# A closing stretch kept in written order: the last blocks of an encoder layer's output stage on four engines

## The chip, the cores and the metric

The kernel runs on one core of a Trainium2 chip. Its engines work side by side, each through its own list of instructions in order: TensorE (PE; its weight loads are PEld), VectorE (DVE), ScalarE (ACT), GpSimd (POOL) and SyncE (SP), which here only issues DMA transfers. Engines wait for one another by semaphores. The metric is the device time of one execution in microseconds (us), the median of several. All times of the trace are in us from the start of the span.

## The reference

One layer of a bidirectional encoder is applied to two sequences of 2048 tokens, 1024 features each, in float32, with shared weights:

```
u = rmsnorm(h, g_norm);  q, k, v, ga, f, gf = split(u @ w_in)
a  = gqa(rope(rmsnorm(q)), rope(rmsnorm(k)), v) * silu(ga)     # 8 q heads, 2 kv heads, 64 wide
fo = (real(fft2(f)) per channel group @ w_fmix) * silu(gf)
h  = h + concat(a, fo) @ w_out
gate = sigmoid(rmsnorm(h, g_ple) @ w_ple_gate)
y  = rmsnorm(h + (p @ w_ple) * gate, g_final)
```

The last three lines are the output stage, and the change is in it.

## The kernel before, in words

Each float32 operand is kept as a high and a low float16 part, and a product is three matmuls per 128 rows of depth: high by high, high by low, low by high (`SPLIT3`). A product of 1024 rows of depth is so a group of 24 matmuls into one bank of PSUM, 128 x 512.

The program first makes the projections, then the attention (`attention`), unit by unit, and between its pieces `interleave` takes pieces of a second stream, `fill`: the rest of the Fourier branch, and then the output stage (`outp`), whose work on the early blocks needs only attention that is already done. A stream is a Python generator; what it yields is the estimated length of the piece it has just written, or `None` for "nothing to be written now". While `interleave` runs, `self.dq` is a list of deferred small steps, written out later by `flush`; when the attention has ended, all of them are written, `self.dq` becomes `None`, and the rest of `fill` is written at once by `drain`.

The output stage works by blocks of 128 tokens, t = 0 to 31 (16 per sequence). For block t there are, by names used from here on:

- the load: `ag` (L1531 and L1532 from the attention's store `agd`, L1533 from the Fourier branch's store `fod`), the gating product on GpSimd (L1535), then the mix as float16, high part `mh` on ScalarE (L1549), low part on VectorE (L1554), and transposes of the Fourier half by DMA, `mT` (L1550). The old features `h` come by L1541.
- out(t,0) and out(t,1): a group of 24 each, `mh` and `mT` against `w_wo`; VectorE adds each to `h` (L1570).
- the norm: `middle(t)` takes the squares of block t and of block t−2 on ScalarE (L1670), one short chain on VectorE gives both roots (L1676 to L1679), then the high part `h_hl` (L1699, ScalarE) and the low part (L1703, VectorE) are transposed by DMA into `hT` (L1700, L1705). Block t−2 gets its last product (L1689) and is stored.
- gate(t,0) and gate(t,1): a group of 24 each, `hT` against `w_pg`; ScalarE's tanh (L1583) reads it.
- emb(t,0) and emb(t,1): the embedding's products, six matmuls, `pT` against `wp`, and two VectorE steps with the tanh (L1592, L1594). They are kept in a list `todo` when the tanh is written, and `embed` writes them at a place inside a later group.

In the interleaved part two groups run at once on half the array each (L1649, tiles of 64 rows): `slot` gives a group its second half beside the next group's first (`halves`). For t >= `WHOLE` = 30, `slot` is called with `whole` true and the group runs alone on the full array (`mm`, L504). A whole group that stands beside a half one is followed by `seen` (L1610), a copy of one column of the half group's bank on VectorE, on which the second half group then waits.

PSUM has eight banks: `ps_f` one, `ps_g` two, and five for the attention, which become `ps_x` when the pool `psD` opens after the attention. `group_bank` takes `ps_x` where that pool is open and `ps_g` otherwise.

The order of instructions on each engine is that of the program text where `tc.manual_schedule` names the engine; elsewhere a scheduler of the language sets it. Before the change, `interleave` runs under a manual schedule for PE, ACT, DVE and SP, and `drain` under the scheduler. GpSimd is under the scheduler in both.

Of the kernel before, what the change touches and what calls it, by code (L numbers as in the profile page):

```python
# [45 lines left out]
_E = mybir.EngineType  # L46
# [119 lines left out]
class Build:  # L166
# [1349 lines left out]
    def outp(self, pool0, ow, open_pool):  # L1516
# [87 lines left out]
        def slot(up, whole):  # L1604


            low = held.pop() if held else None
            def seen():
                j = st.tile([128, 1], F32, name="seen")
                nc.vector.tensor_copy(j[:], low[0][:, 0:1])  # L1610

            if low is not None and low[4] and not whole:
                seen()
            if up is not None and not whole:
                up = (self.group_bank(), *up, not started)
                started.append(True)
                held.append(up)
                yield from halves(up, low)
                return
            if up is not None:  # L1620
                ps = self.group_bank()
                for i, us in enumerate(self.mm(ps[:], up[0], up[1])):
                    yield us
                    yield from embed(i >= 6)
                if low is not None:
                    seen()
                yield from self.after(ticket)
                yield from end(up[2](ps))
            if low is not None:
                yield from halves(None, low)  # L1630

        def embed(now=False):

            if todo and (now or self.dq is None or self.step % 8 in (1, 2, 7)):
                todo.pop()()
                yield 1.48

        def end(more):
            if more is not None:
                todo.append(more)  # L1640
                yield from embed()

        def halves(up, low):
            i = n = 0
            for k in range(8):
                for ia, ib in SPLIT3:
                    for g, sl, a, z in ((up, slice(0, 64), i == 0, False), (low, slice(64, 128), False, i == 23)):
                        if g is not None:
                            nc.tensor.matmul(g[0][:], g[1](ia, k)[sl], g[2](ib, k)[sl], start=a, stop=z,  # L1649
                                             skip_group_check=True)  # L1650
                    i += 1
                    if i in STOPS:
                        yield 0.216 * (i - n)
                        n = i
                        yield from embed(i >= 18)
            yield from self.after(ticket)
            n = self.nflush
            more = low[3](low[0]) if low is not None else None
            yield 0.216 * (24 - STOPS[-1])
            yield from end(more)  # L1660
            if self.dq is not None and self.nflush == n:
                yield None
# [133 lines left out]
        for t in range(N2 + 2):  # L1796
            pr = prep(t + 1) if ok(t + 1) else iter(())
            if ok(t):
                yield from along(slot(out1(t, 0), t >= WHOLE), pr)
                if t == 1:  # L1800
                    yield from middle(0)
                yield from along(slot(out1(t, 1), t >= WHOLE), pr)
                if t == N2 - 2:
                    free.append(True)
                load_p(t)
                M.pop(t)
            if ok(t - 1):
                yield from wait(tk, t - 1)
                yield from along(slot(out3(t - 1, 0), t >= WHOLE), pr)
            if t:  # L1810
                yield from middle(t)
            if ok(t - 1):
                yield from along(slot(out3(t - 1, 1), t >= WHOLE), pr)
            if ok(t + 1):
                if ok(t - 3):
                    yield from wait(t4, t - 3)
                load_x(t + 1)
                yield from pr
                yield from self.after(tm.pop())
# [30 lines left out]
    def run(self):  # L1850
        nc, tc, a = self.nc, self.tc, self.a
# [91 lines left out]
        def fill():  # L1943
            self.nw2k = NW
            self.small = C0 = fill_stack.enter_context(pool("C0", side="right"))
            with pool("B", side="right") as B:
                self.bd = B.tile([128, 2, 512], F32, name="bd")
                ow = {}

                def wload(n, k, pool):  # L1950
                    if k == 0:
                        w = pool.tile([128, 2, 8, 512], F16, name="w_" + n, tag="w16")
                        ow[n] = [w[:, b] for b in range(2)]
                    for b in range(2):
                        nc.sync.dma_start(ow[n][b][:, 2 * k:2 * k + 2, :], self.wd[n][:, b, 2 * k:2 * k + 2, :])

                wl = [lambda n=n, k=k, p=p: wload(n, k, p)
                      for n, p in (("wo0", WP), ("wo1", WP), ("pg0", WP1), ("pg1", WP)) for k in range(4)]
                self.WF.clear()

                calls = []

                def hook(n=1):
                    calls.append(n)
                    for _ in range(n if n > 1 else len(calls) % 2 if len(calls) > 4 else 0):
                        if wl:
                            wl.pop(0)()

                out, go = iter(()), None
                for us in self.fourier2(B, hook):  # L1970
                    if us == "half":
                        out = self.outp(C0, ow, lambda: fill_stack.enter_context(pool("C", side="right")))
                        continue
                    go = go or next(out, None)
                    yield us
                hook(16)
            while not go:
                yield None
                go = next(out)
            yield from out  # L1980

        with tc.manual_schedule(engines={_E.PE, _E.Activation, _E.DVE, _E.SP}):
            f = fill()
# [1 line left out]
        self.step = 10 ** 9  # L1985
        att_stack.close()
        with pool("psD", 5, space=PSUM) as self.psX:
            self.drain(f)
        fill_stack.close()
        w_stack.close()  # L1990

# [52 lines left out]
```

## Time and profile before

| | |
|---|---|
| median of 3 runs | 2601.84 us (2595.85, 2601.84, 2603.52) |
| profiled execution | 2597.87 us, of which the span is 2595.8 us |
| TensorE busy | 2511.0 us, 97% of the span |
| VectorE, ScalarE, GpSimd busy | 1668.4, 1183.6, 1896.6 us |
| granted TensorE clock, mean | 0.991 of full speed |
| part that is no longer interleaved | from about 2507 us to the end |

A row of a timeline has start, duration, engine, line, operation, the tile written and those read, sizes, a count, and in brackets the engine's idle time just before it and what ended it. Equal instructions that follow each other are one row. Matmuls are pipelined: one lasts longer than the distance to the next. L12 is line 12 of the kernel before; in the changed kernel lines from 1608 on stand three or four further down.

### The profile page before, as it was taken

To read this page: it belongs to the slowest core of one execution; us is meant where nothing else is said; L and a number is where in the kernel's file an instruction comes from. 1 tells how busy PE (TensorE), PEld (TensorE's weight loads), DVE (VectorE), ACT (ScalarE), POOL (GpSimd) and SP (SyncE) were. 2 spreads that over 40 slices of the span, in tenths; PEclk is the share of its full clock that TensorE was granted. 3 is DMA by queue.
4 is the path that set the end of the run, shared out by engine and by line. 5 is a ranking of instruction groups with operands and counts; after the bars stand their busy time and mean duration, and the time that the engine had idled before them with its cause. 6 is when DMAs were issued, how large, how long until landed. Compare 5 with 4: busy or idle time off the path is not lost. (4 is left out here: it accounts for less than half of the span.)

```text
span 2595.8 us, 49879 instructions
## 1 busy us (share of the span) xinstructions
PE 2511.0 (97%) x19896; PEld 1384.0 (53%) x19896; DVE 1668.4 (64%) x2382; ACT 1183.6 (46%) x1983; POOL 1896.6 (73%) x1646
## 2 busy tenths in 40 slices
PE   6999989999999999999999999999999999999988
PEld 3566656666656545545545555445544554545533
DVE  7766576777566856566666666666666665766534
ACT  4433353434235545554544545444544444445522
POOL 0465545475659978888888888878887988888840
PEclk9999999999999999999999999999999999999999
DMA  8467588787377742223222233422223322233232
GB/s 259 101 175 198 162 223 230 185 195 180 103 197 248 212 118 62 58 76 78 59 69 75 71 81 88 90 69 63 73 73 82 72 75 63 66 82 76 78 76 53
DMA packets 450265, 297.92 MB, mean 115 GB/s; under 512 B 294000, under 2 KB 394480, under 8 KB 450032
## 3 DMA queue, kind: packets, MB, share of 16 engines
q1 hardware_dynamic: 437952, 256.28, 38.9%
q0 software_dynamic: 12080, 38.46, 4.2%
q8 instruction: 155, 2.54, 0.4%
q14 instruction: 78, 0.64, 0.1%
HBM read 146.12 MB, written 82.45 MB: 88 GB/s over the span
## 5 line engine op out<-in xcount | busy, mean ns | idle before, releaser
L1325 POOL TENSOR_TENSOR acc<-acc,p 128x1024 f32<-128x1024 f32 x384 | 927.6, 2416 | 109.5 <-ACT p L1320 84.6
L1320 ACT ACTIVATE p<-ps_s,s_scale 128x512 f32<-128x512 f32 x1024 | 648.1, 684 | 636.4 <-PE ps_s L1317 613.9
L1355 DVE TENSOR_REDUCE a_mx<-ps_m 128x1 f32<-128x1024 f32 x498 | 608.9, 1223 | 512.0 <-PE ps_m L1347 501.0
L1649 PE MATMUL ps_g<-w_pg,hT 64*128 64x512 f16 x2784 | 494.1, 376 | 3.8 <-DVE seen L1610 2.4
L1383 PE MATMUL ps_o<-p,v 128*64 128x256 f32 x4096 | 468.2, 381 | 0.0
L1317 PE MATMUL ps_s<-q,k 64*128 64x512 f16 x3072 | 433.1, 378 | 1.4 <-ACT p L1320 1.0
L1383 PEld LDWEIGHTS ps_o<-p,v 128*64 128x64 f32 x4096 | 283.7, 137 | 160.4 <-issue 28.5
L504 PEld LDWEIGHTS <-uc 128*128 128x128 f16 x2400 | 236.3, 99 | 231.2 <-DMA uc<-hl 19.5
L1649 PEld LDWEIGHTS <-hT 64*128 64x128 f16 x2784 | 204.8, 94 | 156.9 <-issue 15.7
L1649 PE MATMUL ps_g<-w_wo,mh 64*128 64x512 f16 x1440 | 260.5, 376 | 3.2 <-DVE mh L1554 1.9
L1649 PE MATMUL ps_g<-w_wo,mT 64*128 64x512 f16 x1440 | 257.3, 376 | 0.0
L1317 PEld LDWEIGHTS <-k 64*128 64x128 f16 x3072 | 152.6, 94 | 195.3 <-issue 77.0
L1347 PE MATMUL ps_m<-k,q 64*128 64x512 f16 x996 | 200.8, 377 | 10.2 <-DVE a_mx L1355 9.8
L504 PEld LDWEIGHTS <-w_ga 128*128 128x128 f16 x1536 | 148.8, 98 | 33.5 <-issue 11.9
L1323 POOL TENSOR_TENSOR acc<-p,p 128x1024 f32<-128x1024 f32 x64 | 150.8, 2357 | 11.7 <-ACT p L1320 10.7
L1649 PEld LDWEIGHTS <-mh 64*128 64x128 f16 x1440 | 101.5, 94 | 91.5 <-issue 16.6
L1649 PEld LDWEIGHTS <-mT 64*128 64x128 f16 x1440 | 107.0, 94 | 76.3 <-issue 4.8
L772 POOL TENSOR_TENSOR t<-t,t 128x640 f32<-128x640 f32 x32 | 49.2, 1556 | 121.2 <-DVE t L767 121.2
L1406 DVE RECIPROCAL ps_f<-ps_f 128x256 f32<-128x256 f32 x61 | 107.1, 1756 | 13.6 <-PE ps_f L1399 13.6
L504 PE MATMUL ps_x<-uc,w_ga 128*128 128x256 f16 x1008 | 113.5, 273 | 2.0 <-DVE a_mx L1355 1.4
L504 PE MATMUL ps_x<-w_gf,uc 128*128 128x512 f16 x480 | 108.0, 384 | 2.4 <-DVE a_mx L1355 2.4
L1390 ACT ACTIVATE at<-ps_o,a_scale 128x256 f32<-128x256 f32 x64 | 30.4, 474 | 168.2 <-PE ps_o L1383 168.2
(347 smaller groups left out, 3415.6 us busy)
## 6 DMA issues: line engine op xcount, KB each, us to landing
q<-qTd SPq DMA_DIRECT2D x256, 64.0 KB, 2.2
ag<-agd SPq DMA_DIRECT2D x64, 256.0 KB, 3.5
out<-h POOLq DMA_DIRECT2D x31, 512.0 KB, 3.1
x<-in_x_prompt SPq DMA_DIRECT2D x16, 512.0 KB, 4.9
gfd<-gt POOLq DMA_DIRECT2D x32, 256.0 KB, 2.7
agd<-gat POOLq DMA_DIRECT2D x64, 128.0 KB, 2.8
w_st<-in_w_out SPq DMA_DIRECT2D x32, 256.0 KB, 4.0
w_st<-in_w_ple_gate SPq DMA_DIRECT2D x32, 256.0 KB, 4.0
```

The lines of the kernel that those rows point to most:

```text
L504: self.nc.tensor.matmul(ps, lhs(ia, k), rhs(ib, k), start=(i == 0), stop=(i == 3 * ks - 1))
L772: nc.gpsimd.tensor_tensor(out=t1[:, tt], in0=t1[:, tt], in1=t2[:, tt], op=ALU.add)
L1317: nc.tensor.matmul(S[u][e][:], w[sl], q[sl].rearrange("p h q -> p (h q)"), start=j == i == 0, stop=i + 1 == len(todo), skip_group_check=True)
L1320: nc.scalar.activation(p[:, e, :], S[u][e][:], AF.Exp, scale=self.sc["s_scale"][:])
L1323: nc.gpsimd.tensor_tensor(out=ACC[u][:], in0=P[u, 0][:], in1=p[:], op=ALU.add)
L1325: nc.gpsimd.tensor_tensor(out=ACC[u][:], in0=ACC[u][:], in1=p[:], op=ALU.add)
L1347: nc.tensor.matmul(ps[c], Q[u][0][sl, h, :], kt[s, kv, half][sl, :, 0, :], start=True, stop=True)
L1355: nc.vector.reduce_max(MX[u][:, h, half, c:c + 1], x, axis=AX.X)
L1383: nc.tensor.matmul(o[64 * f:64 * f + 64], vt[s, kv, c // 8][:, c % 8, :], p[:, e, f], start=(c == 0), stop=(c == 15))
L1390: nc.scalar.activation(at[:].rearrange("p c q -> p (c q)"), o, AF.Copy, scale=self.sc["a_scale"][:])
L1406: nc.vector.reciprocal(r, r)
L1649: nc.tensor.matmul(g[0][:], g[1](ia, k)[sl], g[2](ib, k)[sl], start=a, stop=z, skip_group_check=True)
```

## The change

Three edits. `slot` with `whole` true now yields `None` until the interleaved part is over, so that no whole group takes a bank before `psD` is open. Within a whole group, `embed` is asked from the fourth piece on and writes at once (before: at each piece, and at once only from the seventh). And `drain` runs under the manual schedule of the same four engines, so PE, ACT, DVE and SP keep the written order to the end.

```diff
@@ slot @@
             low = held.pop() if held else None
+            while whole and self.dq is not None:
+                yield None
+
             def seen():
@@
                 for i, us in enumerate(self.mm(ps[:], up[0], up[1])):
                     yield us
-                    yield from embed(i >= 6)
+                    if i > 2:
+                        yield from embed(True)
                 if low is not None:
                     seen()
@@ run @@
         with pool("psD", 5, space=PSUM) as self.psX:
-            self.drain(f)
+            with tc.manual_schedule(engines={_E.PE, _E.Activation, _E.DVE, _E.SP}):
+                self.drain(f)
```

No instruction is added or taken away. On every engine the lists are equal up to the end of the interleaved part; GpSimd's is equal throughout. The numbers in names below tell buffers apart.

VectorE at the end of the interleaved part, before. `h_28315`, `h_28738` and `h_28977` are the features of blocks 29, 30 and 31, `h_27780` of block 28, `mh_28865` the mix of block 31:

```order
L1703 SCALAR_TENSOR_TENSOR h_hl_28777<-h_28315,h_r_28677,h_hl_28777 128x1024
L1406 RECIPROCAL ps_m_28698<-ps_m_28698 128x256
L1407 TENSOR_TENSOR at_28595<-at_28595,ps_m_28698 128x256
L1610 COPY seen_28795<-ps_g_28679 128x1
L1554 SCALAR_TENSOR_TENSOR mh_28865<-ag_28744,mix1_s_14957,mh_28865 128x1024
L1570 SCALAR_TENSOR_TENSOR h_28738<-ps_g_28740,mixo10_14961,h_28738 128x512
L1592 SCALAR_TENSOR_TENSOR ps_g_28768<-th_28736,ps_g_28768 128x512
L1594 SCALAR_TENSOR_TENSOR h_27780<-ps_g_28768,p_wp0_7618,h_27780 128x512
```

And VectorE at the same place of the changed kernel (`mh_28867` is the mix of block 31, `h_27152` the features of block 27):

```order
L1707 SCALAR_TENSOR_TENSOR h_hl_28756<-h_28315,h_r_28677,h_hl_28756 128x1024
L1406 RECIPROCAL ps_m_28698<-ps_m_28698 128x256
L1693 SCALAR_TENSOR_TENSOR h_27152<-h_27152,rsh2_z2_28671,gfin_10383 128x1024
L1407 TENSOR_TENSOR at_28595<-at_28595,ps_m_28698 128x256
L1592 SCALAR_TENSOR_TENSOR ps_g_28775<-th_28736,ps_g_28775 128x512
L1594 SCALAR_TENSOR_TENSOR h_27780<-ps_g_28775,p_wp0_7618,h_27780 128x512
L1613 COPY seen_28797<-ps_g_28679 128x1
L1570 SCALAR_TENSOR_TENSOR h_28738<-ps_x_28750,mixo10_14961,h_28738 128x512
L1592 SCALAR_TENSOR_TENSOR ps_g_28826<-th_28824,ps_g_28826 128x512
L1594 SCALAR_TENSOR_TENSOR h_27780<-ps_g_28826,p_wp1_7622,h_27780 128x512
L1570 SCALAR_TENSOR_TENSOR h_28738<-ps_x_28835,mixo11_14963,h_28738 128x512
L1554 SCALAR_TENSOR_TENSOR mh_28867<-ag_28754,mix1_s_14957,mh_28867 128x1024
```

Block 31's low mix (L1554) has gone from ahead of out(30,0)'s read (L1570) to behind out(30,1)'s; `seen` stands behind emb(28,0)'s two steps; block 27's last product (L1689, here L1693) stands behind the reciprocal, not ahead of L1703; and out(30,0) is in a `ps_x` bank. On TensorE, accordingly, the half-array groups are now followed by out(30,0) with emb(28,0) after its twelfth matmul, then the rest of gate(28,1) with 24 matmuls of half the array, emb(28,1), out(30,1), gate(29,0), emb(29,0), gate(29,1), emb(29,1) and out(31,0). Before, one matmul of out(30,1) came first, then three of gate(28,1), all of out(30,0), seven of gate(28,1), emb(28,0), the last fourteen of gate(28,1), emb(28,1), and the other 23 of out(30,1); from gate(29,0) on TensorE's order is the same in both.

SyncE at the same place, before (`hT_28778` is block 29's, `ag_28744` block 31's load, `at_28595` the attention's last unit):

```order
L1700 DMA_TRANSPOSE hT_28778<-h_hl_28777 128x8x128
L1705 DMA_TRANSPOSE hT_28778<-h_hl_28777 128x8x128
L1410 DMA agd1<-at_28595 128x2x128
L1541 DMA h_28738<-in_x_sample 128x1024
L1541 DMA h_28977<-in_x_sample 128x1024
L1531 DMA ag_28744<-agd1 128x4x128
L1532 DMA ag_28744<-agd1 128x4x128
L1533 DMA ag_28744<-fod1 128x512
```

And SyncE at this place of the changed kernel:

```order
L1410 DMA agd1<-at_28595 128x2x128
L1541 DMA h_28738<-in_x_sample 128x1024
L1531 DMA ag_28754<-agd1 128x4x128
L1704 DMA_TRANSPOSE hT_28757<-h_hl_28756 128x8x128
L1709 DMA_TRANSPOSE hT_28757<-h_hl_28756 128x8x128
L1532 DMA ag_28754<-agd1 128x4x128
L1533 DMA ag_28754<-fod1 128x512
```

Block 29's transposes stand behind the attention's last store and the first part of block 31's load; the features of block 31 have left this place, and now come behind block 30's transposes.

ScalarE around the norm of block 31, before (`th_28966` is gate(29,1)'s tanh, `th_29058` gate(30,0)'s, `h_28977` block 31):

```order
L1583 ACTIVATE th_28966<-ps_x_28941,h_pg1_7614 128x512
L1670 ACTIVATE sq_29070,h_ss_29069<-h_28315 128x1024
L1670 ACTIVATE h_hl_29072,h_ss_29069<-h_28977 128x1024
L1699 ACTIVATE h_hl_29099<-h_28977,h_r_29097 128x1024
L1583 ACTIVATE th_29058<-ps_x_29033,h_pg0_7612 128x512
```

And ScalarE at the same place of the changed kernel, where `h_28979` is block 31 and `th_29060` gate(30,0)'s tanh:

```order
L1583 ACTIVATE th_28968<-ps_x_28943,h_pg1_7614 128x512
L1583 ACTIVATE th_29060<-ps_x_29035,h_pg0_7612 128x512
L1674 ACTIVATE sq_29072,h_ss_29071<-h_28315 128x1024
L1674 ACTIVATE h_hl_29074,h_ss_29071<-h_28979 128x1024
L1703 ACTIVATE h_hl_29101<-h_28979,h_r_29099 128x1024
```

Gate(30,0)'s tanh has gone from behind the norm of block 31 to ahead of its squares. VectorE's two steps of emb(30,0) have likewise gone from behind the chain of block 31's norm to ahead of it. The norm of block 30 has changed places with gate(29,0)'s tanh and emb(29,0) in the same way.

## The prediction

> **What bounds the kernel now.** I read the page's engine rows first, then TensorE's timeline from the point where the two orders part, then the granted clock, then VectorE, ScalarE and SyncE for what TensorE waits on. The page:
>
> ```profile
> PE 2511.0 (97%) x19896; PEld 1384.0 (53%) x19896; DVE 1668.4 (64%) x2382; ACT 1183.6 (46%) x1983; POOL 1896.6 (73%) x1646
> ```
>
> TensorE is busy for 97% of the span, so only its idle time and its slow time can be won. The orders part at TensorE's first full-array matmul of the closing stretch, at 2507.05; what stands before is untouched, and so is its time. From there (start, duration, line, tiles, count, idle time and its releaser):
>
> ```profile
> 2507.05 0.39 PE L504 MATMUL ps_x<-w_wo,mh 128*128 128x512 f16 x1
> 2509.87 0.80 PE L1649 MATMUL ps_g<-w_pg,hT 64*128 64x512 f16 x3 [2.42 <-DVE seen L1610]
> 2510.60 4.45 PE L504 MATMUL ps_g<-w_wo,mh 128*128 128x512 f16 x12
> 2514.89 2.75 PE L504 MATMUL ps_g<-w_wo,mT 128*128 128x512 f16 x12
> ...
> 2524.14 2.72 PE L504 MATMUL ps_g<-wp,pT 128*128 128x512 f16 x6 [4.88 <-DVE h L1570]
> ...
> 2530.46 1.47 PE L504 MATMUL ps_g<-wp,pT 128*128 128x512 f16 x6
> ...
> 2536.73 5.34 PE L504 MATMUL ps_x<-w_pg,hT 128*128 128x512 f16 x24
> 2541.91 1.46 PE L504 MATMUL ps_g<-wp,pT 128*128 128x512 f16 x6
> ...
> 2584.64 1.46 PE L504 MATMUL ps_g<-wp,pT 128*128 128x512 f16 x6
> ```
>
> Two gaps, 2.42 and 4.88 us, and slow matmuls behind each; no other row of this stretch has idle time. At full pace 24 matmuls take 2541.91 − 2536.73 = 5.18 us, 0.216 each. The view of busy time by stretches shows the slow ones (stretch, its length, PE busy; third from the end the share of full clock granted):
>
> ```profile
> 374.12:377.53 3.41, 2.10 (x20) 1.64 (x17) 2.83 (x4) 0.72 (x1) 1.92 (x3) 1.00 0.63 209
> 377.53:380.94 3.41, 0.61 (x4) 0.31 (x4) 1.99 (x4) 2.60 (x4) 0.54 (x1) 1.00 0.88 286
> ...
> 2507.45:2510.86 3.41, 0.99 (x5) 0.34 (x6) 2.33 (x4) 0.43 (x1) 0.00 (x0) 1.00 1.08 246
> 2510.86:2514.27 3.41, 3.41 (x10) 1.21 (x9) 0.00 (x0) 0.00 (x0) 0.00 (x0) 0.50 0.92 216
> ...
> 2517.69:2521.10 3.41, 1.57 (x7) 0.56 (x6) 0.00 (x0) 0.14 (x1) 1.26 (x1) 1.00 0.22 71
> 2521.10:2524.51 3.41, 0.37 (x1) 0.10 (x1) 1.95 (x2) 1.01 (x1) 0.00 (x0) 0.50 0.20 38
> ```
>
> A stretch of 3.41 us in which TensorE was busy 0.99 or 1.57 is followed by one at half clock; one with 2.10 busy is not.
>
> **What causes the gaps.** VectorE works strictly in its written order:
>
> ```profile
> 2506.33 1.28 DVE L1703 SCALAR_TENSOR_TENSOR h_hl<-h,h_r,h_hl 128x1024 f16<-128x1024 f32 x1
> 2507.53 1.76 DVE L1406 RECIPROCAL ps_m<-ps_m 128x256 f32<-128x256 f32 x1
> 2509.32 0.42 DVE L1407 TENSOR_TENSOR at<-at,ps_m 128x256 f32<-128x256 f32 x1
> 2509.66 0.15 DVE L1610 COPY seen<-ps_g 128x1 f32<-128x1 f32 x1
> 2522.14 1.28 DVE L1554 SCALAR_TENSOR_TENSOR mh<-ag,mix_s,mh 128x1024 f16<-128x1024 f32 x1 [12.33 <-ACT mh L1549]
> 2523.34 0.74 DVE L1570 SCALAR_TENSOR_TENSOR h<-ps_g,mixo,h 128x512 f32<-128x512 f32 x1
> ```
>
> The copy `seen` stands behind the division (L1406, L1407). The read L1570 of out(30,0) stands behind the low half of block 31's mix (L1554), which waits 12.33 us for a load; that read frees the psG bank in which emb(28,0) is to go.
>
> **The change part by part.**
>
> 1. The old losses. From 2507.05 on there are 11 groups of 24 matmuls and 8 of six, 312, and 312 x 0.216 = 67.3 us. TensorE takes from 2507.05 to 2584.64 + 1.29 = 2585.93, 78.9. The loss is 11.5 us: 2.42 + 4.88 idle; 4.29 − 2.59 = 1.7 on the twelve at 2510.60; (2530.46 − 2524.14) − 20 x 0.216 = 2.0 on the six and fourteen from 2524.14; the rest, 0.5, in single matmuls and drains.
>
> 2. The first gap. Out(30,0) now writes a psX bank and stands first with emb(28,0) inside it, 30 matmuls, 6.5 us, to 2513.5; then the lone gate(28,1). VectorE's list ahead of `seen` gets longer: L1703 still starts at 2506.33 when ScalarE is done, then 1.2 + 1.76, then L1689, new in this place (1.28, by L1554's row of the same shape), then 0.4 for L1407, then L1592 and L1594 (0.74 each, by L1570's row of the same shape), which end at 2512.5. Emb(28,0) is done by 2511.0, when L1592 wants it. `seen` ends near 2512.6, 0.9 us before TensorE asks. Cost nothing, covered by out(30,0); without that cover about 1 us and a half-clock stretch.
>
> 3. The second gap. L1570 now stands ahead of L1554, out groups use five psX banks, and emb groups need only a bank that L1594 or a tanh has left. L1554 still waits for block 31, but TensorE reaches block 31 only 144 matmuls on, at 2538.1. Cost nothing.
>
> 4. SyncE's queue. Store, loads and transposes change places:
>
> ```profile
> 2510.87 0.53 SPq L1410 DMA_DIRECT2D agd<-at  x1
> 2511.50 0.92 SPq L1541 DMA_DIRECT2D h<-in_x_sample  x2
> 2513.09 0.38 SPq L1531 DMA_DIRECT2D ag<-agd  x1
> ...
> 2519.67 1.26 POOL L1535 TENSOR_TENSOR ag<-ag 128x512 f32<-128x512 f32 x1 [12.58 <-DMA ag<-agd]
> ```
>
> L1407 moves from 2509.3 to about 2510.6, so the store to 2511.05. L1531 needs its landing, 2513.3. Only then go both transposes of block 29 (1.24 each), to 2516.2, and only then L1532 and L1533. Block 29's hT is wanted after 84 matmuls, 2525.2; with the slowest landing of any hT, 7.2 us (row below), it is there at 2522.2. The load took 6.6 us from L1531 to the product; from 2516.3 that is 2522.9, then 1.26 + 1.15 + 1.28 and a transpose with 3.1: 2531, seven before 2538.1. The second half of `L1541 x2` goes behind block 30's transposes, to about 2540, and even with 6.6 us it lands ahead of out(31,1)'s end at 2548.5. All cost nothing, hidden by gates and outs of blocks 29 and 30; past that cover each us costs one.
>
> 5. The new wait. Block 31's norm used to follow out(31,1) directly. In written order, `middle(31)` first issues emb(30,0) and its two VectorE steps, and ScalarE does tanh(30,0) before the squares. The steps as they last now, and the time from issue to landing, of all hT transposes of the run, and of block 31's second alone:
>
> ```profile
> 2571.90 0.69 ACT L1583 ACTIVATE th<-ps_x,h_pg 128x512 f32<-128x512 f32 x1 [5.35 <-PE ps_x L504]
> 2562.21 0.17 DVE L1676 TENSOR_SCALAR h_ms<-h_ss 128x2 f32<-128x2 f32 x1 [1.22 <-ACT h_hl L1670]
> 2564.82 1.15 ACT L1699 ACTIVATE h_hl<-h,h_r 128x1024 f16<-128x1024 f32 x1 [2.65 <-DVE h_r L1679]
> 2566.00 1.24 SPq L1700 DMA_TRANSPOSE hT<-h_hl  x1
> 2567.34 1.28 SPq L1705 DMA_TRANSPOSE hT<-h_hl  x1
> DMA to landing us min/median/max: 3.0/3.1/7.2
> hT<-h_hl SPq DMA_TRANSPOSE x1, 4.9
> ```
>
> Let W be the start of emb(30,0), 216 matmuls on, 2553.7. A gate's last matmul ends 0.16 past the next group's start (2536.73 + 5.34 against 2541.91), so tanh runs from W + 0.2 to W + 0.9; two squares over 128x1024, 1.15 each by L1699's row, end at W + 3.2, and VectorE's two steps for emb(30,0) (W + 1.3 + 0.2 + 2 x 0.74) at W + 3.0; h_ms to L1699 2.61, W + 5.8; first transpose 1.18 later, W + 7.0; the second 1.34 later, W + 8.35; landings at 3.1: W + 10.1 and W + 11.45. TensorE has 6 + 24 + 6 matmuls until gate(31,0), W + 7.8, and can do two on the first half alone, 0.43. It loses 11.45 − 7.8 − 0.4 = 3.25 us. Bounds: 3.15 (landing 3.0) to 5.05 (4.9, as the second transpose of block 31 took beside an output store; I take 3.1, since that store, L1689, now comes behind L1703). Block 30 has the same chain, with 48 matmuls (10.4 us) more to hide it: nothing.
>
> 6. The clock behind the new wait. 3.25 us idle within 3.7 mostly leave one stretch under 1.6 busy, so half clock follows: none to 1.7 us (as behind the 2.42 gap), by where the stretches fall; I take 1.2.
>
> [...]
>
> Sum: −11.5 + 3.25 + 1.2 = −7.1 us. The last steps after 2586 (squares, norm, final product, store) are the same. The profiled execution is 2597.87 in all with a span of 2595.8, so it becomes 2590.8, span 2588.7. The shown median is 2601.84, 4.0 above that execution; the same 7.1 off it gives **2594.7**. That is 0.27%, and about 0.3% (7.8 us) is what a measurement of this kernel can tell from no change.
>
> **The rivals.**
>
> A. The clock stays full behind the new wait: −8.3, 2593.5. For it: idle time split by two matmuls over two stretches. Against: 3.25 us rarely divide so evenly. Chance 0.12. [...]
>
> B. The new wait or `seen` is worse: transposes at 4.9, half clock in full, or VectorE 1 us late: −11.5 + 5.05 + 1.7 + 1 = −3.8, 2598. For: 4.9 was measured in this very place. Chance 0.20.
>
> C. No new wait: ScalarE's chain hides after all; −11.5, 2590.3. Against: 11.45 against 7.8 is far. Chance 0.06.
>
> D. Slower: block 29's transposes, now behind the store and its reload in SyncE's queue, land late, and gate(29,0) waits at 2525.2. It decides past 2532.3 (the 7.1 used up); at 2541 the time would be 2610. For: one order, four transfers ahead. Against: needs 17 us where 7.2 was the longest. Chance 0.05.
>
> E. The change does not do what it says: the gaps return at other instructions, 2602. Chance 0.04.
>
> **How the numbers follow.** The forecast holds 0.53. Its own range is −4.8 (5.05 and 1.7) to −8.4 (3.15 and no clock loss). The three times shown spread from 2595.85 to 2603.52, so a median may lie 2 or 3 us off; 2588 to 2600 takes in C in part, A and B. Faster by over 0.3%: a little under half of the forecast 0.25, most of A and C 0.14, a fifth of B and a bit of E 0.05: 0.44. Slower: D and a trace of E, 0.06. Same 0.50.
>
> **What would show it.** TensorE's timeline after 2507 without the gaps of `seen` and L1570, gate(29,0) starting near 2525; one new gap of 2 to 3.5 us ahead of the last gate(31,0), released by the hT transposes, with matmuls near 0.43 us behind it; end of emb(31,1) near 2578.8. Wrong if a gap stands before 2553, or if the new gap is under 1 or over 5.

## The result and the profile after

The changed kernel took 2592.29 us (median of 20 runs, 2586.20 to 2602.52), the kernel before in the same comparison 2601.08 us (20 runs, 2595.82 to 2607.77). The ratio is 0.997, 95% interval 0.9961 to 0.9979, so 0.2 to 0.4% less. The forecast was 2594.7 within 2588 to 2600; the median lies in that range, and the forecast change of 0.27% lies inside the interval.

The profiled execution took 2593.99 us with a span of 2591.9 us. TensorE's timeline of the changed kernel, from the first matmul of out(30,0) to the last group (start, duration, line, tiles, count, idle time and its releaser; lines from 1608 on stand three or four further down than before):

```profile
2510.16 2.76 PE L504 MATMUL ps_x<-w_wo,mh 128*128 128x512 f16 x12
2512.76 1.46 PE L504 MATMUL ps_g<-wp,pT 128*128 128x512 f16 x6
2514.06 2.75 PE L504 MATMUL ps_x<-w_wo,mT 128*128 128x512 f16 x12
2516.74 5.35 PE L1653 MATMUL ps_g<-w_pg,hT 64*128 64x512 f16 x24
2522.03 1.47 PE L504 MATMUL ps_g<-wp,pT 128*128 128x512 f16 x6
...
2557.00 1.46 PE L504 MATMUL ps_g<-wp,pT 128*128 128x512 f16 x6
2558.30 5.34 PE L504 MATMUL ps_x<-w_pg,hT 128*128 128x512 f16 x24
2563.48 1.46 PE L504 MATMUL ps_g<-wp,pT 128*128 128x512 f16 x6
2567.01 0.79 PE L504 MATMUL ps_x<-w_pg,hT 128*128 128x512 f16 x2 [2.08 <-DMA hT<-h_hl]
2568.35 6.07 PE L504 MATMUL ps_x<-w_pg,hT 128*128 128x512 f16 x22 [0.56 <-DMA hT<-h_hl]
2574.26 1.46 PE L504 MATMUL ps_g<-wp,pT 128*128 128x512 f16 x6
```

The gaps of 2.42 us (`seen`) and 4.88 us (L1570) are gone; no row of this stretch has idle time before 2567. One new gap stands ahead of gate(31,0), in two pieces, both ended by the transposes of block 31, and the 22 matmuls behind it take 2574.26 − 2568.35 = 5.91 us instead of 4.75, which is 22 at the full pace of 0.216.

In this execution the closing stretch begins 3.1 us later than in the one before (2510.16 against 2507.05), though TensorE's list up to there is the same: that is the spread between executions. So the stretch from out(30,0)'s first matmul to the end of the span is compared: 2595.8 − 2507.05 = 88.7 us before, 2591.9 − 2510.16 = 81.7 us after, 7.0 less. This figure is used for every run below.

VectorE at the beginning of the stretch, changed kernel:

```profile
2515.07 0.75 DVE L1594 SCALAR_TENSOR_TENSOR h<-ps_g,p_wp,h 128x512 f32<-128x512 f32 x1
2515.73 0.15 DVE L1613 COPY seen<-ps_g 128x1 f32<-128x1 f32 x1
2519.81 0.75 DVE L1570 SCALAR_TENSOR_TENSOR h<-ps_x,mixo,h 128x512 f32<-128x512 f32 x1 [3.92 <-DMA h<-in_x_sample]
2523.61 0.70 DVE L1592 SCALAR_TENSOR_TENSOR ps_g<-th,ps_g 128x512 f32<-128x512 f32 x1 [3.05 <-PE ps_g L504]
2528.71 0.75 DVE L1570 SCALAR_TENSOR_TENSOR h<-ps_x,mixo,h 128x512 f32<-128x512 f32 x1 [3.62 <-PE ps_x L504]
2529.38 1.27 DVE L1554 SCALAR_TENSOR_TENSOR mh<-ag,mix_s,mh 128x1024 f16<-128x1024 f32 x1
...
2547.82 0.75 DVE L1570 SCALAR_TENSOR_TENSOR h<-ps_x,mixo,h 128x512 f32<-128x512 f32 x1 [3.46 <-DMA h<-in_x_sample]
```

`seen` ends at 2515.88, and TensorE asks at 2516.74. The low mix of block 31 (L1554) still comes late, but behind both reads of block 30, and nothing on TensorE waits for it. The last row is the read of out(31,0), which waits for the features of block 31.

The chain that ends in the new gap, on ScalarE, VectorE and SyncE:

```profile
2557.20 0.69 ACT L1583 ACTIVATE th<-ps_x,h_pg 128x512 f32<-128x512 f32 x1 [16.15 <-PE ps_x L504]
2557.79 1.05 ACT L1674 ACTIVATE sq<-h 128x1024 f16<-128x1024 f32 x1
2558.83 1.04 ACT L1674 ACTIVATE h_hl<-h 128x1024 f16<-128x1024 f32 x1
2559.30 0.75 DVE L1594 SCALAR_TENSOR_TENSOR h<-ps_g,p_wp,h 128x512 f32<-128x512 f32 x1
2560.00 0.17 DVE L1680 TENSOR_SCALAR h_ms<-h_ss 128x2 f32<-128x2 f32 x1
2562.60 1.15 ACT L1703 ACTIVATE h_hl<-h,h_r 128x1024 f16<-128x1024 f32 x1 [2.64 <-DVE h_r L1683]
2563.78 1.24 SPq L1704 DMA_TRANSPOSE hT<-h_hl  x1
2565.12 1.28 SPq L1709 DMA_TRANSPOSE hT<-h_hl  x1
```

Out(31,1) was read at 2552.0. ScalarE's squares stand behind gate(30,0)'s tanh until 2557.8 and VectorE's chain (from L1680) behind emb(30,0)'s two steps until 2560.0; the two end within 0.2 us of each other. The transposes land 3.2 us after their issue, and TensorE goes on at 2567.0 and 2568.35. And the clock (stretch, its length, PE busy first; third from the end the granted share):

```profile
2563.91:2567.32 3.41, 1.33 (x7) 0.41 (x5) 3.37 (x4) 0.46 (x1) 0.16 (x1) 1.00 0.73 135
2567.32:2570.73 3.41, 2.85 (x8) 0.87 (x7) 0.34 (x1) 0.00 (x0) 0.37 (x1) 0.50 0.49 173
```

A stretch with 1.33 us busy, and then one at half clock.

### The profile page after: what moved, and what is told of

Same layout as the page of the kernel before. It is cut to its first block, busy times and chain, and to the rows that moved or that the text cites. A ratio compares the mean times of both kernels' runs of the same rounds, so it can differ in the third digit from the quotient of the medians.

```text
span 2591.9 us, 49880 instructions
## 1 busy us (share of the span) xinstructions
PE 2510.8 (97%) x19896; PEld 1384.8 (53%) x19896; DVE 1662.2 (64%) x2382; ACT 1183.2 (46%) x1983; POOL 1898.4 (73%) x1646
## 5 line engine op out<-in xcount | busy, mean ns | idle before, releaser
L1653 PEld LDWEIGHTS <-hT 64*128 64x128 f16 x2784 | 204.8, 94 | 153.6 <-issue 11.5
L1323 POOL TENSOR_TENSOR acc<-p,p 128x1024 f32<-128x1024 f32 x64 | 150.9, 2358 | 10.1 <-ACT p L1320 9.3
```

The lines of the kernel that those rows point to most:

```text
L1323: nc.gpsimd.tensor_tensor(out=ACC[u][:], in0=P[u, 0][:], in1=p[:], op=ALU.add)
```

## The experiments

The theory was that each gap goes with an instruction's place in a list, that everything else moved is covered, and that the new gap is the place of block 31's norm plus what the clock adds. The main rivals were that the psX banks made the whole gain and the kept order only costs, that the transposes themselves are slow there, and that any step added to VectorE's list shows.

### The first two edits, without the kept order

```diff
         with pool("psD", 5, space=PSUM) as self.psX:
-            with tc.manual_schedule(engines={_E.PE, _E.Activation, _E.DVE, _E.SP}):
-                self.drain(f)
+            self.drain(f)
```

> The first two edits alone: whole groups begin in the last pool and the products stand at the fourth piece, but the closing stretch is ordered by the scheduler again. TensorE's list is then that of the changed kernel; VectorE's has block 31's low mix between the two steps of emb(28,0), and block 31's norm directly behind out(31,1). Theory (each gap goes with its place in the list): no wait for seen; no wait for hT before gate(31,0); but emb(28,1) waits for the bank that emb(28,0)'s second step frees, behind block 31's load, so one gap of 4 to 6 us near 12 us after the stretch begins, with half clock behind it. Closing stretch (from out(30,0)'s first matmul to the end of the span) 88.7 - 2.4 - 1.7 - 0.5 = about 84, between before (88.7) and the changed kernel (81.7); time about 4 us below before. Rival (the banks make the gain and the kept order only costs): the gap of 4.88 goes with the psX bank, the new wait goes too, and the stretch is about 77.5, time 11 us below before.

Measured: median 2593.44 us (11 runs) against 2600.44 before (17 runs), ratio 0.9967, interval 0.9954 to 0.998. TensorE and VectorE of this kernel:

```profile
2508.03 2.76 PE L504 MATMUL ps_x<-w_wo,mh 128*128 128x512 f16 x12
...
2523.30 2.72 PE L504 MATMUL ps_g<-wp,pT 128*128 128x512 f16 x6 [3.34 <-DVE h L1594]
2525.82 3.16 PE L504 MATMUL ps_x<-w_wo,mh 128*128 128x512 f16 x12
2528.81 2.75 PE L504 MATMUL ps_x<-w_wo,mT 128*128 128x512 f16 x12
```

```profile
2512.20 0.70 DVE L1592 SCALAR_TENSOR_TENSOR ps_g<-th,ps_g 128x512 f32<-128x512 f32 x1 [1.41 <-PE ps_g L504]
2521.31 1.28 DVE L1554 SCALAR_TENSOR_TENSOR mh<-ag,mix_s,mh 128x1024 f16<-128x1024 f32 x1 [8.41 <-ACT mh L1549]
2522.51 0.74 DVE L1594 SCALAR_TENSOR_TENSOR h<-ps_g,p_wp,h 128x512 f32<-128x512 f32 x1
2523.17 0.74 DVE L1570 SCALAR_TENSOR_TENSOR h<-ps_x,mixo,h 128x512 f32<-128x512 f32 x1
```

The stretch is 2590.4 − 2508.03 = 82.4 us; about 84 was expected. As the theory had it, the gap of `seen` is gone, there is no wait for `hT`, and one gap stays, ahead of emb(28,1), because L1594 stands behind block 31's low mix. It is 3.34 us, less than the 4 to 6 expected: in this order two of block 31's three loads stand ahead of the attention's last store, and its GpSimd product starts 10.8 us into the stretch (2518.83), not 12.6 (2519.67 before). The 18 slow matmuls behind it cost (2528.81 − 2523.30) − 18 x 0.216 = 1.6 us, and 77.4, the stretch of the versions below that have no gap, and 3.34 and 1.6 make 82.3. The rival's 77.5 did not come.

Both old gaps are gone here without the kept order. The read of out(30,0) (L1570, last row) still stands behind block 31's low mix, but it frees a `ps_x` bank for which nothing waits; what waits now is a `ps_g` bank behind L1594. So each of the two orders has one gap, at a different place and of nearly the same price: in these profiles the stretches differ by 0.7 us, of which 0.2 lies in the gap (3.34 against 81.7 − 1.2 − 77.4 = 3.1 in the changed kernel) and 0.4 in the slow matmuls (1.6 against 1.2).

### The norm of block 31 ahead of gate(30,0)

```diff
+            early = t == N2 - 1
+            if early:
+                yield from middle(t)
             if ok(t - 1):
                 yield from wait(tk, t - 1)
                 yield from along(slot(out3(t - 1, 0), t >= WHOLE), pr)
-            if t:
+            if t and not early:
                 yield from middle(t)
```

> The changed kernel with the norm of block 31 written ahead of gate(30,0), so that its chain starts when out(31,1) is read and has 60 more matmuls' time (13 us) to end. Theory (the wait before gate(31,0) is the norm's place in the list): both waits for hT, 2.08 and 0.56 us, and the half-clock stretch behind them are gone, TensorE has no idle time from out(30,0) to emb(31,1); closing stretch 67.4 + 9.7 + under 0.5 = 77.5 instead of 81.7; time 4 us below the changed kernel, 12 below before (ratio to before 0.9955). Rival (the transposes themselves are what is slow there, or another engine takes the wait over, such as ScalarE with the tanh of gate(30,0) queued behind the norm): a gap of over 1 us remains somewhere in the stretch and it stays above 79.

Measured: median 2586.82 us (6 runs) against 2600.44, ratio 0.9953, interval 0.994 to 0.9967. TensorE's first and last groups of the stretch:

```profile
2505.80 2.76 PE L504 MATMUL ps_x<-w_wo,mh 128*128 128x512 f16 x12
...
2559.12 1.46 PE L504 MATMUL ps_g<-wp,pT 128*128 128x512 f16 x6
2560.41 5.34 PE L504 MATMUL ps_x<-w_pg,hT 128*128 128x512 f16 x24
...
2572.07 1.46 PE L504 MATMUL ps_g<-wp,pT 128*128 128x512 f16 x6
```

No idle time is left; from 2505.80 to the begin of the last group are 66.27 us for 306 matmuls, 0.217 each, full pace. The stretch is 2583.2 − 2505.80 = 77.4 us, expected 77.5. The norm's place in the list was the whole of the new gap. The stretch is 4.3 us shorter than the changed kernel's. The median is the lowest so far, but it was not taken beside the changed kernel; the last experiment compares its near twin, with both norms moved, with the changed kernel on one chip.

### A longer norm, in block 31 and in block 30

```diff
             e.tensor_scalar(out=q[:], in0=r[:, 0:1], scalar1=U_SC, scalar2=None, op0=ALU.mult)
+            for _ in range(8 if t == N2 - 1 else 0):     # N2 - 2 in the second
+                e.tensor_scalar(out=q[:], in0=q[:], scalar1=1.0, scalar2=None, op0=ALU.mult)
```

> The changed kernel with eight more small steps (a multiplication by one of 128x1 each, about 0.195 us) in block 31's norm, between the root and the high part: the chain to gate(31,0) is 1.6 us longer and nothing else is. Theory: the gap before gate(31,0) grows from 2.08 to about 3.7 us, and the closing stretch from 81.7 by 1.6 (by up to 0.6 more or less where the half-clock stretch falls) to about 83.3. Rival (the wait is set by something else that ends at that time, such as the transposes' queue): the gap stays at 2.1.

> The same eight steps, but in block 30's norm, whose transposes are wanted 48 matmuls later. Theory (its chain is covered by out(31,0) and out(31,1)): no gap before gate(30,0), closing stretch 81.7 as in the changed kernel, within the 0.6 us of the clock. Rival (VectorE as a whole is what sets the pace there, so any step added to its list shows): about 83.3, as with the same steps in block 31.

Each was executed once (2592.21 us in block 31, 2591.28 in block 30), so only the stretches are compared. In block 31 the gap grows by what was added (3.60 + 0.64 against 2.08 + 0.56), and the stretch is 2590.1 − 2506.43 = 83.7 us:

```profile
2506.43 2.76 PE L504 MATMUL ps_x<-w_wo,mh 128*128 128x512 f16 x12
...
2564.81 0.60 PE L504 MATMUL ps_x<-w_pg,hT 128*128 128x512 f16 x2 [3.60 <-DMA hT<-h_hl]
2566.05 6.61 PE L504 MATMUL ps_x<-w_pg,hT 128*128 128x512 f16 x22 [0.64 <-DMA hT<-h_hl]
```

In block 30 no gap stands ahead of gate(30,0), and the one of block 31 is as it was:

```profile
2508.71 2.76 PE L504 MATMUL ps_x<-w_wo,mh 128*128 128x512 f16 x12
...
2550.37 5.34 PE L504 MATMUL ps_x<-w_pg,hT 128*128 128x512 f16 x24
...
2565.65 0.61 PE L504 MATMUL ps_x<-w_pg,hT 128*128 128x512 f16 x2 [2.17 <-DMA hT<-h_hl]
2566.83 4.92 PE L504 MATMUL ps_x<-w_pg,hT 128*128 128x512 f16 x22 [0.57 <-DMA hT<-h_hl]
```

The stretch is 2589.2 − 2508.71 = 80.5 us, 1.2 less than the changed kernel's, where no more than 0.6 either way was expected. That is the clock: the 22 matmuls take 4.75 us here, 5.91 in the changed kernel's profile. The granted clock stayed full (stretch, its length, PE busy first; third from the end the granted share):

```profile
2561.36:2564.77 3.41, 2.12 (x10) 0.78 (x8) 2.43 (x3) 1.55 (x2) 0.00 (x0) 1.00 0.40 74
2564.77:2568.19 3.42, 1.97 (x9) 0.78 (x10) 1.41 (x3) 0.00 (x0) 0.53 (x1) 1.00 0.81 233
```

The same gap fell across the end of a stretch, and each of the two stretches was left 1.97 us or more busy. With the time over full pace on the 22 matmuls taken off (83.7 − 1.7 = 82.0, 80.5 − 0.0, and 81.7 − 1.2 = 80.5 in the changed kernel), the eight steps cost 1.5 us where the chain is open and nothing where 48 more matmuls cover it, and VectorE as a whole does not set the pace there.

### Without the second edit

```diff
                     yield us
-                    if i > 2:
-                        yield from embed(True)
+                    yield from embed(i >= 6)
```

> The first and the third edit, without the second: the old line of the products, which in the closing stretch writes them after the first piece of out(30,0) (three matmuls) and no longer after the fourth (twelve). Theory (the fourth piece is only there to let gate(28,0)'s tanh end first): the three matmuls take 0.65 us and the tanh ends about 0.8 us after the stretch begins, so emb(28,0) waits 0.1 to 0.3 us; seen is earlier or the same; everything else as in the changed kernel, stretch 81.7 plus 0.2, or 80.5 where the clock stays full behind the wait for hT. Rival (the place of the products is part of the gain): a gap of over 1 us near the begin of the stretch, and half clock behind it.

```profile
2508.29 0.82 PE L504 MATMUL ps_x<-w_wo,mh 128*128 128x512 f16 x3
2509.14 1.46 PE L504 MATMUL ps_g<-wp,pT 128*128 128x512 f16 x6
2510.43 2.10 PE L504 MATMUL ps_x<-w_wo,mh 128*128 128x512 f16 x9
```

Emb(28,0) begins 0.85 us after out(30,0), where three matmuls take 0.65: a wait of 0.2 us. The stretch of the one execution (2592.68 us) is 2590.6 − 2508.29 = 82.3 us; the 22 matmuls behind the wait for `hT` (2.09 and 0.61) take 6.45, 1.7 more than at full pace, and 80.5 + 0.2 + 1.7 is 82.4. The fourth piece is worth 0.2 us.

The third edit alone, the kept order without the banks, was not run. By the program text, emb(28,0) would then be written inside out(30,0) and want one of two psG banks, both held by groups that end later in the same list, so TensorE could not go on; that is argued, not shown.

### Both norms moved, and the changed kernel once more

The first differs from the kernel above in `early = WHOLE <= t < N2`; the second is the changed kernel as it is. Both ran on one chip.

> The changed kernel with the norms of blocks 30 and 31 both written ahead of the gates of the block before; in the run before only block 31's was. Theory (block 30's norm has cover either way): stretch 77.4 as with block 31's norm alone, no idle time, ratio to before 0.995. Rival (block 31's mix, which now stands behind block 30's norm on ScalarE and behind its transposes on SyncE, comes late): a gap ahead of out(31,0).

> The changed kernel once more, beside the one with both norms moved, on the same chip. Theory: waits for hT of 2.1 and 0.6 us as in its first trace; the loss to the clock behind them is 0 to 1.7 us and not the same in each trace, since it goes with where the stretches of 3.41 us fall (0.0 in one of the traces so far, 1.2 and 1.7 in two); stretch 80.5 to 82.2; time 3 to 4.5 us above the kernel with both norms moved. Rival (the clock loss belongs to the wait): 1.2 us again, stretch 81.7.

Measured, against 2599.66 us before (17 runs): both norms moved 2587.44 us (6 runs), ratio 0.9956, interval 0.9941 to 0.9972; the changed kernel 2592.40 us (12 runs), ratio 0.9979, interval 0.9968 to 0.999. The stretches are 2585.0 − 2507.64 = 77.4 us, without idle time, and 2595.2 − 2513.28 = 81.9 us:

```profile
2570.16 0.60 PE L504 MATMUL ps_x<-w_pg,hT 128*128 128x512 f16 x2 [2.10 <-DMA hT<-h_hl]
2571.36 6.33 PE L504 MATMUL ps_x<-w_pg,hT 128*128 128x512 f16 x22 [0.60 <-DMA hT<-h_hl]
2577.53 1.46 PE L504 MATMUL ps_g<-wp,pT 128*128 128x512 f16 x6
```

The waits are the same to 0.1 us and the 22 matmuls behind them take 6.17 − 4.75 = 1.4 us over full pace, a fourth value. The stretches differ by 4.5 us and the medians by 5.0, where 3 to 4.5 was expected; the slowest run with both norms moved (2589.39) is below the fastest of the changed kernel (2590.36). Block 30's norm gains nothing by being earlier: it had cover.

| kernel | closing stretch, us | idle time of TensorE in it, us | slow matmuls behind it, us over full pace |
|---|---|---|---|
| before | 88.7 | 2.42 + 4.88 | 1.7 + 2.0 |
| changed | 81.7 | 2.08 + 0.56 | 1.2 |
| changed, once more | 81.9 | 2.10 + 0.60 | 1.4 |
| first two edits | 82.4 | 3.34 | 1.6 |
| without the second edit | 82.3 | 2.09 + 0.61 | 1.7 |
| norm 31 longer | 83.7 | 3.60 + 0.64 | 1.7 |
| norm 30 longer | 80.5 | 2.17 + 0.57 | 0.0 |
| norm 31 first | 77.4 | none | none |
| both norms first | 77.4 | none | none |

## Why the prediction was right

1. The old losses, 11.5 us. The two versions with moved norms have no gap and no slow matmul, and their stretch of 77.4 is 11.3 less than before. So this term was the true ceiling. (312 x 0.216 is 67.4, not 67.3; it changes the loss by under 0.1.)

2. The first gap. Predicted to vanish, with `seen` 0.9 us ahead of TensorE; measured 0.86 (2515.88 against 2516.74). The step that is new in this place of VectorE's list, L1689 (here L1693), kept it 1.1 us and not 1.28, but then L1592 waited 0.5 for emb(28,0)'s matmuls; the two nearly cancel. The run with the first two edits alone has the same cover on TensorE, and no wait for `seen` either.

3. The second gap. Predicted to vanish since L1570 stands ahead of L1554 and out groups use psX banks. It did. The run with the first two edits alone parts the two reasons. The bank is enough for this gap: there L1570 still stands behind L1554, and nothing waits for it. But the bank alone does not empty the stretch: L1554 then stands ahead of L1594, which frees a psG bank, and a gap of 3.34 us opens. What the kept order adds is that L1554 stands behind the steps of emb(28,0) and emb(28,1) and the reads of block 30; when its turn comes, at 2529.38, the load is there and it holds nothing up.

4. SyncE's queue, all at nothing. Gate(29,0) started on time with the transposes of block 29 issued at 2516.3 and 2518.1, the first landing 5.2 us later and the second not later than that, so by 2523.3; they are wanted 84 matmuls into the stretch, 2528.3. Their sizes differ: each transpose kept the queue for 1.7 and 2.2 us and not 1.24, and the load was then faster, its product starting at 2523.70, 13.5 us into the stretch (15.8 predicted). That these terms cost nothing was right, but two waits were not seen. The features of block 30 (L1541) stand behind the attention's store in both kernels, but out(30,0)'s read no longer stands behind L1554 and wants them earlier: VectorE is idle 3.92 us until they land. It was idle 3.05 us more before its next step. And the features of block 31 were held against out(31,1)'s end, while out(31,0)'s read wants them first: issued at 2543.21, they let it start at 2547.82, 1.0 us after out(31,0)'s last matmul ended at 2546.8. TensorE waited for neither.

5. The new wait. Predicted: first half landing at W + 10.1, second at W + 11.45, a loss of 3.25 us without the clock. W is 2557.00, TensorE went on at 2567.01 and 2568.35, that is W + 10.0 and W + 11.35; a start at W + 7.8 and two matmuls off, the loss is 3.1. The first transpose was issued at W + 6.8, 0.2 earlier than predicted, and landed 3.2 later and not 3.1. The longer norm and the moved norm confirm that this chain sets it.

6. The clock, 1.2 us taken between none and 1.7. On the 22 matmuls four executions with this wait measured 1.2, 1.4, 1.7 and 0.0 us over full pace, and the one with the longer wait 1.7. The bounds were both met. That the profile of the changed kernel hit 1.2 itself is luck, as the price goes with the execution.

The sum was −7.1, against −7.0 in the profiles and −8.8 between the medians, which carry the spread of the part before the stretch: its begin lay between 2505.80 and 2513.28 us in nine profiles with the same list of TensorE up to there. An agreement to 0.1 us is closer than the clock term allows, and so luck. The prediction took 0.3% as the least that a measurement can tell from no change; with 20 runs a side the interval is 0.2 to 0.4%, so this change is told from none.

The rivals: A (the clock stays full) happened in one of the four executions with this wait, with the idle time divided over two stretches, so it is one end of the term and not another outcome. B needed landings of 4.9, and 3.2 was measured, the first with no other packet in flight when it was issued (none from 2563.7 to 2564). C's 77.4 exists, but only with the norm moved. D's transposes took 5.2 us, not 17. E's gaps at other instructions came once, ahead of gate(31,0), as forecast, and not at the old price.

What the prediction did not see: that the scheduler, given the first two edits, reaches nearly the same time. These two make 6.3 of the 7.0 us, and the kept order adds 0.7 by one profile each, less than the 0.0 to 1.7 by which the slow matmuls vary between executions, and nothing that the medians can tell (ratios 0.9967 and 0.997).

## What to carry to other kernels

Where engines work strictly in the written order, read for each wait of the bounding engine what stands ahead of its releaser in the releaser's list: here a step that waited 12.33 us for a load (L1554, before) held back the read behind it, and with it a bank for which TensorE waited 4.88 us. When an order is replaced as a whole, lay the two lists of each engine beside each other to the end and time every chain that has moved against the matmuls that are left to cover it; here that gave both the gain and the new gap, and the new gap named the next edit (a few lines, 4.3 us off the stretch). And compare the stretch in which the change acts, as two whole times of this kernel differ by more than the change (2586.20 to 2602.52 us in 20 runs, against 7.0).

## What the runs showed of the hardware that was not expected

Two waits of nearly one length were not followed by the same clock. In the changed kernel 2.6 us of idle time (2.08 + 0.56) left the stretch from 2563.91 busy for 1.33 us, and half clock followed (0.50); with norm 30 longer 2.7 us (2.17 + 0.57) were divided so that two stretches had 2.12 and 1.97, and the clock stayed at 1.00. In the closing stretches of these traces the busiest stretch of 3.41 us that was followed by half clock had 1.57 us (before, 2517.69), and the least busy that was not had 1.76 (norm 31 longer, 2559.44 to 2562.85). Earlier in the program the busy time does not part the two. The changed kernel, earlier in its trace:

```profile
959.63:963.04 3.41, 2.03 (x14) 0.64 (x13) 2.91 (x3) 2.50 (x5) 3.41 (x2) 1.00 0.52 97
963.04:966.45 3.41, 3.41 (x18) 1.92 (x20) 1.29 (x2) 0.38 (x1) 3.25 (x3) 0.50 0.60 131
```

And the kernel with norm 31 first:

```profile
767.66:771.07 3.41, 1.48 (x10) 1.35 (x10) 1.51 (x2) 1.44 (x3) 2.36 (x2) 1.00 1.01 369
771.07:774.48 3.41, 3.41 (x28) 2.01 (x26) 1.66 (x2) 2.37 (x6) 3.36 (x3) 1.00 0.97 338
```

With 2.03 us busy half clock followed, and with 1.48 it did not. So the busy time that the profile shows does not alone tell which clock follows; what else counts is open.

The stretches fall differently against the program from trace to trace. In the changed kernel's the edge at 2567.32 lies 0.3 us behind the begin of gate(31,0) (2567.01), and with norm 30 longer the edge at 2564.77 lies 0.9 us ahead of it (2565.65). The same wait cost 0.0, 1.2, 1.4 and 1.7 us in four executions.
